# A batched matmul minus a tensor: transfers of two tiles in one fixed order, stores trailing, transposes between the matmuls

## The chip, the cores and the metric

The kernel runs on one core of one Trainium2 chip. The metric is the time on the device in microseconds (us). A kernel's time is the median of its runs. The profile is of one execution.

## The reference

```python
batch, m, k, n = 16, 512, 1024, 768      # x [16,512,1024], weight [1024,768], sub_value [16,512,768], all float32

def reference(x, weight, sub_value):
    return (np.matmul(x, weight) - sub_value).astype(np.float32)
```

The batch and m are flattened: 8192 rows of x, each with 1024 elements, times one weight, less 8192 rows of sub_value. In all 33.55 MB of x, 3.15 MB of weight and 25.17 MB of sub_value are read, and 25.17 MB are written.

## The kernel before

The 8192 rows are cut into 64 tiles of 128 rows. A tile goes through five steps:

- x is loaded as float32 (`load_x_sup`, L76), one DMA for four tiles. Each partition holds four successive rows of x, so a DMA moves 16 KB a partition, 2 MB in all.
- ScalarE casts one tile to float16 (`do_cast`, L104).
- TensorE transposes it in eight blocks of 128 x 128 into a PSUM tile (`do_transpose`, L112), and ScalarE copies that to SBUF as `xt_tile` (L117).
- TensorE multiplies `xt_tile` by the weight (`do_matmul`, L127): first 512 columns of the result, eight matmuls, one for each 128 of k, then the other 256 columns, eight more.
- VectorE subtracts `sub_tile` from the PSUM result into `out_tile` (L136). Once four tiles are done, one DMA stores them (L143). `sub_tile` is loaded by one DMA for four tiles too (L83).

The weight is loaded in eight pieces of 128 rows (L88) through two staging buffers, and VectorE casts each to float16 (L89). All DMAs are issued by SP, and SP takes its instructions in order: where one waits, those behind it wait as well.

The loop runs over the tiles. In it, casts run nine tiles ahead of the matmuls (`C_AHEAD`), transposes six (`T_AHEAD`) and x loads three groups of four (`X_AHEAD`), as far as the buffers allow. The order that the engines get is not quite that of the code: the framework's scheduler places each instruction when it thinks it can run, so weight loads and x loads are mixed on SP, and the transposes of several tiles are put together on TensorE. The framework also gives each DMA one of eight semaphores in turn (`DMAHW0` to `DMAHW7`); a DMA may have to wait for the one that last used the same semaphore, as some rows below show.

Of the kernel before, what the change touches and what calls it, by code (L numbers as in the profile page):

```python
# [1 line left out]

# [5 lines left out]

P = 128
F32 = mybir.dt.float32  # L10
F16 = mybir.dt.float16


@with_exitstack
def kernel(
    ctx: ExitStack,
    tc: tile.TileContext,
    x: bass.AP,
    weight: bass.AP,
    sub_value: bass.AP,  # L20
    out: bass.AP,
):
    nc = tc.nc

    x_flat = x.flatten_outer_dims()
    sub_flat = sub_value.flatten_outer_dims()
    out_flat = out.flatten_outer_dims()

    M_TOT, K = x_flat.shape
    _, N = weight.shape  # L30
    assert M_TOT % P == 0
    assert K % P == 0
    n_mtiles = M_TOT // P
    n_ktiles = K // P

    SUP = 4
    assert n_mtiles % SUP == 0
    n_sup = n_mtiles // SUP

    x_sup_ap = x_flat.rearrange("(s p j) k -> s p j k", p=P, j=SUP)  # L40
    sub_sup_ap = sub_flat.rearrange("(s p j) n -> s p j n", p=P, j=SUP)
    out_sup_ap = out_flat.rearrange("(s p j) n -> s p j n", p=P, j=SUP)

    n_splits = []
    n0 = 0
    while n0 < N:
        w = min(512, N - n0)
        n_splits.append((n0, w))
        n0 += w

    T_AHEAD = 6
    C_AHEAD = 9
    X_AHEAD = 3

    const_pool = ctx.enter_context(tc.tile_pool(name="const", bufs=1))
    w_stage_pool = ctx.enter_context(tc.tile_pool(name="w_stage", bufs=2))
    w_pool = ctx.enter_context(tc.tile_pool(name="w_pool", bufs=1))
    x_pool = ctx.enter_context(tc.tile_pool(name="x_pool", bufs=X_AHEAD + 1))
    x16_pool = ctx.enter_context(tc.tile_pool(name="x16_pool", bufs=6))
    xt_pool = ctx.enter_context(tc.tile_pool(name="xt_pool", bufs=T_AHEAD + 2))  # L60
    sub_pool = ctx.enter_context(tc.tile_pool(name="sub_pool", bufs=3))
    out_pool = ctx.enter_context(tc.tile_pool(name="out_pool", bufs=2))
    psum_t_pool = ctx.enter_context(tc.tile_pool(name="psum_t", bufs=4, space=bass.MemoryType.PSUM))
    psum_o_pool = ctx.enter_context(tc.tile_pool(name="psum_o", bufs=2, space=bass.MemoryType.PSUM))

    identity = const_pool.tile([P, P], F16)
    make_identity(nc, identity)

    w_sb = w_pool.tile([P, n_ktiles, N], F16)

    x_tiles: dict[int, bass.AP] = {}

    def load_x_sup(s):
        t = x_pool.tile([P, SUP, K], F32, tag="x", name="x_tile")
        x_tiles[s] = t
        nc.sync.dma_start(out=t, in_=x_sup_ap[s])  # L76

    sub_tiles: dict[int, bass.AP] = {}

    def load_sub_sup(s):  # L80
        t = sub_pool.tile([P, SUP, N], F32, tag="sub", name="sub_tile")
        sub_tiles[s] = t
        nc.sync.dma_start(out=t, in_=sub_sup_ap[s])  # L83

    load_x_sup(0)
    for kt in range(n_ktiles):
        w_stage = w_stage_pool.tile([P, N], F32, name="w_stage")
        nc.sync.dma_start(out=w_stage, in_=weight[kt * P : (kt + 1) * P, :])  # L88
        nc.vector.tensor_copy(out=w_sb[:, kt], in_=w_stage)  # L89
    for s in range(1, X_AHEAD + 1):  # L90
        if s < n_sup:
            load_x_sup(s)
    load_sub_sup(0)
    if n_sup > 1:
        load_sub_sup(1)

    x16_tiles: dict[int, bass.AP] = {}
    xt_tiles: dict[int, bass.AP] = {}

    def do_cast(mi):  # L100
        s, j = divmod(mi, SUP)
        t = x16_pool.tile([P, K], F16, name="x16_tile")
        x16_tiles[mi] = t
        nc.scalar.copy(out=t, in_=x_tiles[s][:, j])  # L104

    def do_transpose(mi):
        x16_tile = x16_tiles.pop(mi)
        xt_tile = xt_pool.tile([P, n_ktiles, P], F16, name="xt_tile")
        xt_tiles[mi] = xt_tile
        psum_t = psum_t_pool.tile([P, n_ktiles, P], F16, name="psum_t")  # L110
        for kt in range(n_ktiles):
            nc.tensor.transpose(  # L112
                psum_t[:, kt, :],
                x16_tile[:, kt * P : (kt + 1) * P],
                identity,
            )
        nc.scalar.copy(out=xt_tile, in_=psum_t)  # L117

    out_tiles: dict[int, bass.AP] = {}

    def do_matmul(mi):
        s, j = divmod(mi, SUP)
        xt_tile = xt_tiles.pop(mi)
        psum_o = psum_o_pool.tile([P, N], F32, name="psum_o")
        for n0, nw in n_splits:
            for kt in range(n_ktiles):
                nc.tensor.matmul(  # L127
                    psum_o[:, n0 : n0 + nw],
                    xt_tile[:, kt, :],
                    w_sb[:, kt, n0 : n0 + nw],  # L130
                    start=(kt == 0),
                    stop=(kt == n_ktiles - 1),
                )
        if j == 0:
            out_tiles[s] = out_pool.tile([P, SUP, N], F32, name="out_tile")
        nc.vector.tensor_tensor(  # L136
            out=out_tiles[s][:, j],
            in0=psum_o,
            in1=sub_tiles[s][:, j],
            op=mybir.AluOpType.subtract,  # L140
        )
        if j == SUP - 1:
            nc.sync.dma_start(out=out_sup_ap[s], in_=out_tiles.pop(s))  # L143

    for mi in range(min(C_AHEAD, n_mtiles)):
        do_cast(mi)
    for mi in range(min(T_AHEAD, n_mtiles)):
        do_transpose(mi)

    for mi in range(n_mtiles):  # L150
        s, j = divmod(mi, SUP)
        if j == 0:
            if s + X_AHEAD + 1 < n_sup:
                load_x_sup(s + X_AHEAD + 1)
            if s + 2 < n_sup:
                load_sub_sup(s + 2)
        if mi + C_AHEAD < n_mtiles:
            do_cast(mi + C_AHEAD)
        if mi + T_AHEAD < n_mtiles:
            do_transpose(mi + T_AHEAD)  # L160
        do_matmul(mi)


# [1 line left out]
_INS = ['x', 'weight', 'sub_value']  # L165
_OUTS = [((16, 512, 768), 'float32')]


# [23 lines left out]
```

## Time and profile before

| | |
|---|---|
| runs | 228.85, 230.29, 231.27 us; median 230.29 |
| profiled execution: span from first to last instruction | 229.0 us (its own time is not listed beside the three; the median stands 1.3 us above the span) |
| TensorE matmuls | 203.4 us busy, 89% of the span |
| ScalarE / VectorE | 124.0 us (54%) / 65.8 us (29%) |
| DMA | 87.04 MB on SP's queue, its packets 91.1% of 16 engines' span |

Lines of the profile name an engine (PE is TensorE, PEld its weight loads, DVE VectorE, ACT ScalarE, SPq the DMA issues of SP), a line of the kernel and the tiles. A row of the chain of waits has its start in us, its length in us, and what ran; xN says how many instructions are merged. A row of a table of windows has the stretch (from:to and its length), the busy us and instructions of PE, PEld, DVE, ACT and POOL, and at its end the clock that TensorE was granted (1.00 is full), the busy share of the DMA engines and the GB/s that they moved. A row of instructions grouped by line has the busy us, the mean ns of one, the idle us before them and what ended that.

### The profile page before, as it was taken

To read this page: it belongs to the slowest core of one execution; us is meant where nothing else is said; L and a number is where in the kernel's file an instruction comes from. 1 tells how busy PE (TensorE), PEld (TensorE's weight loads), DVE (VectorE), ACT (ScalarE), POOL (GpSimd) and SP (SyncE) were. 2 spreads that over 40 slices of the span, in tenths; PEclk is the share of its full clock that TensorE was granted. 3 is DMA by queue.
4 is the path that set the end of the run, shared out by engine and by line. 5 is a ranking of instruction groups with operands and counts; after the bars stand their busy time and mean duration, and the time that the engine had idled before them with its cause. 6 is when DMAs were issued, how large, how long until landed. Compare 5 with 4: busy or idle time off the path is not lost.

```text
span 229.0 us, 3465 instructions
## 1 busy us (share of the span) xinstructions
PE 203.4 (89%) x1536; PEld 132.6 (58%) x1536; DVE 65.8 (29%) x72; ACT 124.0 (54%) x129; POOL 0.7 (0%) x6
## 2 busy tenths in 40 slices
PE   0259559999999999999999999999999999999970
PEld 0236325666666676666757576667575766666540
DVE  0101113333333331423332413333332413233430
ACT  2499863382583666566583939475656565510000
POOL 1000000000000000000000000000000000000000
PEclk9995967999999999999999999999999999999996
DMA  6999999999999999999999999999999999750606
GB/s 235 421 429 401 427 431 432 419 399 412 352 427 427 439 419 433 425 436 420 430 429 431 423 424 426 431 426 423 429 423 435 424 416 350 305 240 39 271 6 275
DMA packets 8079, 87.26 MB, mean 381 GB/s; under 512 B 896, under 2 KB 896, under 8 KB 1920
## 3 DMA queue, kind: packets, MB, share of 16 engines
q1 hardware_dynamic: 8064, 87.04, 91.1%
q8 instruction: 12, 0.20, 0.3%
q14 instruction: 3, 0.02, 0.0%
HBM read 61.87 MB, written 25.17 MB: 380 GB/s over the span
## 4 chain that ended last, share of the span: by engine, by line
PE 82%; DMA 12%; DVE 1%; ACT 0%; SPq 0%; issue 0%
PE psum_o L127 72%; DMA w_stage<-in_weight_dram 12%; PE psum_t L112 10%; DVE w_sb L89 1%; ACT xt_tile L117 0%; DVE out_tile L136 0%; SPq L88 0%; SPq L76 0%
## 5 line engine op out<-in xcount | busy, mean ns | idle before, releaser
L127 PE MATMUL psum_o<-w_sb,xt_tile 128*128 128x512 f16 (+1 forms) x1024 | 174.7, 330 | 3.6 <-DVE w_sb L89 3.1
L127 PEld LDWEIGHTS <-xt_tile 128*128 128x128 f16 x1024 | 100.1, 99 | 70.3 <-issue 4.6
L117 ACT COPY xt_tile<-psum_t 128x1024 f16<-128x1024 f16 x64 | 63.2, 1016 | 68.9 <-PE psum_t L112 37.6
L136 DVE TENSOR_TENSOR out_tile<-psum_o,sub_tile 128x768 f32<-128x768 f32 x64 | 61.3, 958 | 129.4 <-PE psum_o L127 126.2
L104 ACT CAST x_tile<-x_tile 128x1024 f16<-128x1024 f32 x64 | 63.5, 1053 | 8.8 <-DMA x_tile<-in_x_dram 8.8
L112 PE MATMUL psum_t<-identity,x_tile 128*128 128x128 f16 x512 | 37.4, 230 | 15.1 <-ACT x_tile L104 14.6
L112 PEld LDWEIGHTS <-x_tile 128*128 128x128 f16 x512 | 33.7, 104 | 19.0 <-ACT x_tile L104 16.1
L89 DVE CAST w_sb<-w_stage 128x768 f16<-128x768 f32 x8 | 4.5, 560 | 27.9 <-DMA w_stage<-in_weight_dram 27.9
L104 ACT ACT_TABLE_LOAD x1 | 1.3, 1283 | 0.7 <-PEq L176 0.7
masks.py:199 POOL TENSOR_SCALAR_AFFINE_SELECT identity<-identity 128x128 f16<-128x128 f16 x1 | 0.3, 294 | 0.1
masks.py:197 POOL MEMSET identity<- 128x128 f16 x1 | 0.2, 205 | 0.3 <-POOLq L176 0.3
L176 POOL MEMSET const-bfloat16-1.0<- 128x1 bf16 x1 | 0.1, 102 | 0.0
L176 POOL MEMSET const-uint8-127<- 128x1 uint8 x1 | 0.1, 102 | 0.0
L176 POOL MEMSET const-float32-0.0<- 128x1 f32 x1 | 0.1, 99 | 0.2 <-issue 0.2
L176 POOL MEMSET const-float32-1.0<- 128x1 f32 x1 | 0.1, 99 | 0.0
## 6 DMA issues: line engine op xcount, KB each, us to landing
x_tile<-in_x_dram SPq DMA_DIRECT2D x16, 2048.0 KB, 14.6
sub_tile<-in_sub_value_dram SPq DMA_DIRECT2D x16, 1536.0 KB, 17.8
out_dram<-out_tile SPq DMA_DIRECT2D x16, 1536.0 KB, 10.1
w_stage<-in_weight_dram SPq DMA_DIRECT2D x8, 384.0 KB, 6.3
```

The costliest lines, as they stand in the source:

```text
L89: nc.vector.tensor_copy(out=w_sb[:, kt], in_=w_stage)
L104: nc.scalar.copy(out=t, in_=x_tiles[s][:, j])
L112: nc.tensor.transpose(psum_t[:, kt, :], x16_tile[:, kt * P : (kt + 1) * P], identity,)
L117: nc.scalar.copy(out=xt_tile, in_=psum_t)
L127: nc.tensor.matmul(psum_o[:, n0 : n0 + nw], xt_tile[:, kt, :], w_sb[:, kt, n0 : n0 + nw], start=(kt == 0), stop=(kt == n_ktiles - 1),)
L136: nc.vector.tensor_tensor(out=out_tiles[s][:, j], in0=psum_o, in1=sub_tiles[s][:, j], op=mybir.AluOpType.subtract,)
L176: nc = _bacc.Bacc("TRN2", target_bir_lowering=False, num_devices=1)
```

## The change

A group is now two tiles (`J = 2`), for x, sub and out alike, so a DMA moves 1 MB of x or 0.79 MB of sub or out. The weight is loaded in four pieces of 256 rows (0.79 MB), with as many staging buffers; a partition holds two successive rows of the weight, so block `kt` of k consists of every second row of a piece, and the transposes read every second column of the cast x to match. At the start SP issues x tile 0, weight piece 0, x tile 1 and the other weight pieces, then groups 1 and 2 of x, and so on. For each group g, `transfers(g)` then issues the x load of group g+4, the sub load of g+2 and the store of g-2, in this order. The result is written over `so_tile`, which held sub. The matmuls make 384 + 384 columns in two PSUM banks, both halves for one block of k after each other, and after each such pair one transpose of the tile two ahead follows. Each instruction is wrapped in `keep`, which holds it in the order of the code.

```diff
+J = 2
+D = 6
+TA = 2
+CA = 2
...
-    x_pool = ctx.enter_context(tc.tile_pool(name="x_pool", bufs=X_AHEAD + 1))
-    x16_pool = ctx.enter_context(tc.tile_pool(name="x16_pool", bufs=6))
-    xt_pool = ctx.enter_context(tc.tile_pool(name="xt_pool", bufs=T_AHEAD + 2))
-    sub_pool = ctx.enter_context(tc.tile_pool(name="sub_pool", bufs=3))
-    out_pool = ctx.enter_context(tc.tile_pool(name="out_pool", bufs=2))
-    psum_t_pool = ctx.enter_context(tc.tile_pool(name="psum_t", bufs=4, space=bass.MemoryType.PSUM))
-    psum_o_pool = ctx.enter_context(tc.tile_pool(name="psum_o", bufs=2, space=bass.MemoryType.PSUM))
+    x_pool = ctx.enter_context(tc.tile_pool(name="x_pool", bufs=6))
+    x16_pool = ctx.enter_context(tc.tile_pool(name="x16_pool", bufs=4))
+    xt_pool = ctx.enter_context(tc.tile_pool(name="xt_pool", bufs=4))
+    so_pool = ctx.enter_context(tc.tile_pool(name="so_pool", bufs=11))
+    psum_t_pool = ctx.enter_context(tc.tile_pool(name="psum_t", bufs=2, space=bass.MemoryType.PSUM))
+    psum_o_pool = ctx.enter_context(tc.tile_pool(name="psum_o", bufs=3, space=bass.MemoryType.PSUM))
...
+    def load_w(c):
+        st = w_stage_pool.tile([P, 2, N], F32, name="w_stage")
+        keep(nc.sync.dma_start(out=st, in_=w_c[c]))
+        keep(nc.vector.tensor_copy(out=w_sb[:, c], in_=st))
...
+                c, r = divmod(kt, 2)
+                keep(nc.tensor.transpose(
+                    ps_t[mi][:, kt * P : (kt + 1) * P],
+                    x16_t[mi][:, 2 * P * c + r : 2 * P * (c + 1) : 2],
+                    ident,
+                ))
...
+                for h in range(2):
+                    keep(nc.tensor.matmul(
+                        po_t[mi][:, h, :NS],
+                        lhsT,
+                        w_sb[:, c, r, h * NS : (h + 1) * NS],
+                        start=(kt == 0),
+                        stop=(kt == n_kt - 1),
+                    ))
...
+    def finish(mi):
+        g, j = divmod(mi, J)
+        o = so_t[g][:, j].rearrange("p (h n) -> p h n", h=2)
+        keep(nc.vector.tensor_tensor(
+            out=o, in0=po_t.pop(mi)[:, :, :NS], in1=o, op=mybir.AluOpType.subtract
+        ))
+    load_x(0, 0)
+    load_w(0)
+    load_x(0, 1)
+    for c in range(1, n_c):
+        load_w(c)
+    load_x(1)
+    load_x(2)
+    load_sub(0)
+    load_x(3)
+    load_sub(1)
+    def transfers(g):
+        if g + 4 < n_g:
+            load_x(g + 4)
+        if g + 2 < n_g:
+            load_sub(g + 2)
+        if g - (D - 4) >= 0:
+            store(g - (D - 4))
...
+    for mi in range(n_mt):
+        if mi % J == 0:
+            transfers(mi // J)
+        mm = matmuls(mi)
+        tr = transposes(mi + TA) if mi + TA < n_mt else []
+        per = max(1, n_kt // len(tr)) if tr else 1
+        for kt in range(n_kt):
+            mm[kt]()
+            if tr and kt % per == per - 1:
+                tr.pop(0)()
+        if mi + CA + TA < n_mt:
+            cast(mi + CA + TA)
+        finish(mi)
+    for g in range(n_g - (D - 4), n_g):
+        store(g)
```

SP at the start of the program, before the change. Numbers tell buffers apart; 128x4096 are four tiles of x, 128x768 one of the eight weight pieces, and what a DMA waits for stands in brackets:

```order
L76 DMA x_tile_91<-in_x_dram 128x4096
L88 DMA w_stage_93<-in_weight_dram 128x768
L88 DMA w_stage_96<-in_weight_dram 128x768
L76 DMA x_tile_117<-in_x_dram 128x4096
L88 DMA w_stage_99<-in_weight_dram 128x768 [waits DMAHW1_49,DVE_49]
L88 DMA w_stage_102<-in_weight_dram 128x768 [waits DMAHW2_49,DVE_49]
L76 DMA x_tile_119<-in_x_dram 128x4096
L88 DMA w_stage_105<-in_weight_dram 128x768 [waits DMAHW4_49,DVE_49]
```

The same place after the change; 128x1536 is one of the four weight pieces, or a group of sub:

```order
L82 DMA x_tile_88<-in_x_dram 128x1024
L73 DMA w_stage_90<-in_weight_dram 128x1536
L82 DMA x_tile_88<-in_x_dram 128x1024
L73 DMA w_stage_94<-in_weight_dram 128x1536
L73 DMA w_stage_97<-in_weight_dram 128x1536
L73 DMA w_stage_100<-in_weight_dram 128x1536
L80 DMA x_tile_103<-in_x_dram 128x2048
L80 DMA x_tile_105<-in_x_dram 128x2048
L86 DMA so_tile_107<-in_sub_value_dram 128x1536 [waits DMAHW0_49]
```

The whole weight moved ahead of the second group of x, and no weight load waits any more. From the ninth DMA on, each waits for the one eight before it.

SP further on after the change, where the first stores stand (before the change, the first store stands behind five x loads of four tiles and three sub loads):

```order
L80 DMA x_tile_275<-in_x_dram 128x2048 [waits DMAHW7_49,Activation_49]
L86 DMA so_tile_277<-in_sub_value_dram 128x1536 [waits DMAHW0_49]
L89 DMA out_0_dram<-so_tile_107 128x1536 [waits DMAHW1_49,DVE_49]
L80 DMA x_tile_342<-in_x_dram 128x2048 [waits DMAHW2_49,Activation_49]
L86 DMA so_tile_344<-in_sub_value_dram 128x1536 [waits DMAHW3_49]
L89 DMA out_0_dram<-so_tile_111 128x1536 [waits DMAHW4_49,DVE_49]
```

The x load of group 6 (`x_tile_275`) stands ahead of the store of group 0, and that of group 7 behind it.

TensorE where the first matmuls stand, before the change (`x16_tile` is the cast x, `psum_t` receives transposes, `psum_o` the result; LDWEIGHTS loads the stationary operand):

```order
L112 LDWEIGHTS x16_tile_133
L112 MATMUL psum_t_179<-identity_85,x16_tile_133 128x128
L127 LDWEIGHTS xt_tile_145 [waits Activation_49]
L127 MATMUL psum_o_228<-w_sb_90,xt_tile_145 128x512 [waits DVE_49]
L127 LDWEIGHTS xt_tile_145
L127 MATMUL psum_o_228<-w_sb_90,xt_tile_145 128x512 [waits DVE_49]
L127 LDWEIGHTS xt_tile_156 [waits Activation_49]
L127 MATMUL psum_o_260<-w_sb_90,xt_tile_156 128x512
```

The same place after the change:

```order
L111 LDWEIGHTS x16_tile_126
L111 MATMUL psum_t_128<-ident_82,x16_tile_126 128x128
L130 LDWEIGHTS xt_tile_124
L130 MATMUL psum_o_147<-w_sb_87,xt_tile_124 128x384 [waits DVE_49]
L130 LDWEIGHTS xt_tile_124
L130 MATMUL psum_o_147<-w_sb_87,xt_tile_124 128x384
L111 LDWEIGHTS x16_tile_139 [waits Activation_49]
L111 MATMUL psum_t_150<-ident_82,x16_tile_139 128x128 [waits PE_49]
```

Before, four tiles are transposed ahead and the first two are then multiplied in turn; now two are transposed ahead, and after two matmuls of tile 0 comes a transpose of tile 2 (`x16_tile_139`, cast from `x_tile_103`, which is group 1 of x). This pattern of two matmuls and one transpose goes on to tile 61.

More of the change, by code (lines that the diff above doesn't have):

```diff
@@ L23 @@
     nc = tc.nc
+    keep = tc.keep_in_program_order
     x_flat = x.flatten_outer_dims()
@@ L30 @@
     _, N = weight.shape
[L31 to L49, printed above, removed]
@@ L64 @@
-    psum_o_pool = ctx.enter_context(tc.tile_pool(name="psum_o", bufs=2, space=bass.MemoryType.PSUM))
[L66 to L101, printed above, removed]
-        t = x16_pool.tile([P, K], F16, name="x16_tile")
-        x16_tiles[mi] = t
-        nc.scalar.copy(out=t, in_=x_tiles[s][:, j])
@@ L106, in do_transpose @@
[L106 to L161, printed above, removed]
+    x_pool = ctx.enter_context(tc.tile_pool(name="x_pool", bufs=6))
@@ new lines @@
+    x16_pool = ctx.enter_context(tc.tile_pool(name="x16_pool", bufs=4))
[3 more added lines that the diff above has]
+    psum_o_pool = ctx.enter_context(tc.tile_pool(name="psum_o", bufs=3, space=bass.MemoryType.PSUM))
+    ident = const_pool.tile([P, P], F16)
+    make_identity(nc, ident)
+    w_sb = w_pool.tile([P, n_c, 2, N], F16)
@@ new lines, with load_x @@
+    x_t = {}
+    so_t = {}
+    x16_t = {}
+    xt_t = {}
+    ps_t = {}
+    po_t = {}
+    def load_w(c):
+        st = w_stage_pool.tile([P, 2, N], F32, name="w_stage")
+        keep(nc.sync.dma_start(out=st, in_=w_c[c]))
+        keep(nc.vector.tensor_copy(out=w_sb[:, c], in_=st))
+    def load_x(g, js=None):
+        if g not in x_t:
+            x_t[g] = x_pool.tile([P, J, K], F32, name="x_tile")
+        if js is None:
+            keep(nc.sync.dma_start(out=x_t[g], in_=x_g[g]))
+        else:
+            keep(nc.sync.dma_start(out=x_t[g][:, js], in_=x_g[g][:, js]))
@@ new lines, in load_sub, with store, cast, transposes @@
+    def load_sub(g):
+        so_t[g] = so_pool.tile([P, J, N], F32, name="so_tile")
+        keep(nc.sync.dma_start(out=so_t[g], in_=sub_g[g]))
+    def store(g):
+        keep(nc.sync.dma_start(out=out_g[g], in_=so_t.pop(g)))
+    def cast(mi):
+        g, j = divmod(mi, J)
+        t = x16_pool.tile([P, K], F16, name="x16_tile")
+        x16_t[mi] = t
+        keep(nc.scalar.copy(out=t, in_=x_t[g][:, j]))
+    def transposes(mi):
+        def start():
+            ps_t[mi] = psum_t_pool.tile([P, K], F16, name="psum_t")
+        def fin():
+            xt = xt_pool.tile([P, K], F16, name="xt_tile")
+            xt_t[mi] = xt
+            keep(nc.scalar.copy(out=xt, in_=ps_t.pop(mi)))
+            x16_t.pop(mi)
+        def one(kt):
+            def f():
+                if kt == 0:
+                    start()
+                c, r = divmod(kt, 2)
[4 more added lines that the diff above has]
+                ))
+                if kt == n_kt - 1:
+                    fin()
+            return f
+        return [one(kt) for kt in range(n_kt)]
@@ new lines, in matmuls, with one, f @@
+    def matmuls(mi):
+        def one(kt):
+            def f():
+                if kt == 0:
+                    po_t[mi] = psum_o_pool.tile([P, 2, 512], F32, name="psum_o")
+                c, r = divmod(kt, 2)
+                lhsT = xt_t[mi][:, kt * P : (kt + 1) * P]
+                for h in range(2):
[6 more added lines that the diff above has]
+                    ))
+            return f
+        return [one(kt) for kt in range(n_kt)]
@@ new lines, in finish @@
+    def finish(mi):
+        g, j = divmod(mi, J)
+        o = so_t[g][:, j].rearrange("p (h n) -> p h n", h=2)
[19 more added lines that the diff above has]
+            store(g - (D - 4))
@@ new lines @@
+    for mi in range(TA):
+        cast(mi)
+        for f in transposes(mi):
+            f()
+    for mi in range(TA, CA + TA):
+        cast(mi)
+    for mi in range(n_mt):
[11 more added lines that the diff above has]
+        finish(mi)
```

14 lines of the change are left out of this document (10 added, 4 removed).

## The prediction

> **What bounds the kernel now.** I read the page first, then the chain that ended last in order of time, then the waits and the start of the timeline.
>
> ```profile
> span 229.0 us, 3465 instructions
> PE 203.4 (89%) x1536; PEld 132.6 (58%) x1536; DVE 65.8 (29%) x72; ACT 124.0 (54%) x129; POOL 0.7 (0%) x6
> q1 hardware_dynamic: 8064, 87.04, 91.1%
> PE psum_o L127 72%; DMA w_stage<-in_weight_dram 12%; PE psum_t L112 10%; DVE w_sb L89 1%; ACT xt_tile L117 0%; DVE out_tile L136 0%; SPq L88 0%; SPq L76 0%
> ```
>
> TensorE and the transfers are both near full; the chain lies on TensorE for 82% and on the weight's DMA for 12%. In order of time the chain shows where each is:
>
> ```profile
> 1.64 9.14 DMA w_stage<-in_weight_dram
> ...
> 11.40 6.25 DMA w_stage<-in_weight_dram
> ...
> 18.26 6.26 DMA w_stage<-in_weight_dram
> ...
> 25.13 6.69 DMA w_stage<-in_weight_dram
> 31.85 0.57 DVE w_sb L89
> 32.46 4.44 PE psum_o L127 x18
> ...
> 54.20 0.45 PE psum_t L112 x8
> 54.64 2.60 PE psum_o L127 x16
> ...
> 182.16 1.79 PE psum_t L112 x32
> 183.94 10.40 PE psum_o L127 x64
> ...
> 196.13 26.02 PE psum_o L127 x160
> 222.17 0.96 DVE out_tile L136
> ```
>
> SP's own waits name what holds the weight back:
>
> ```profile
> SPq L88 <- DMA w_stage<-in_weight_dram: 15.9, 3, 7.0
> ```
>
> Until 31.85 us the weight arrives in pairs of 384 KB, each pair waiting on SP for a staging buffer, with a 2 MB x load queued ahead of it. From 32.46 to 222.17 TensorE hardly stops. A tile (128 rows of the result) costs 0.45 + 2.60 = 3.05 us; four at a time cost 1.79 + 10.40 = 12.19, so 3.048 each. All 64 tiles need 195.1 us, and TensorE ends at 222.17: **27.1 us of start-up loss**. The steady part is at the price of its columns (16 matmuls of 384 columns on average, 162.5 ns each; transposes 56 ns each), so the change must win at the start, at the end, or not at all.
>
> **The change, part by part.**
>
> *Start.* What the weight and x cost to arrive is read from the first casts and from the transfer windows:
>
> ```profile
> 8.89 3.88 ACT L104 CAST x_tile<-x_tile 128x1024 f16<-128x1024 f32 x4 [6.87 <-DMA x_tile<-in_x_dram]
> 10.81 0.56 DVE L89 CAST w_sb<-w_stage 128x768 f16<-128x768 f32 x1 [0.40 <-DMA w_stage<-in_weight_dram]
> 16.70 0.56 DVE L89 CAST w_sb<-w_stage 128x768 f16<-128x768 f32 x1 [5.33 <-DMA w_stage<-in_weight_dram]
> 2.00:26.00 24.00, 11.26 (x84) 7.87 (x85) 3.36 (x6) 17.13 (x20) 0.00 (x0) 0.86 0.99 409
> 26.00:46.00 20.00, 16.02 (x108) 9.91 (x107) 4.95 (x6) 9.57 (x10) 0.00 (x0) 0.83 1.00 422
> 46.00:62.00 16.00, 16.00 (x115) 10.04 (x114) 5.75 (x6) 8.90 (x10) 0.00 (x0) 1.00 1.00 384
> 62.00:178.00 116.00, 116.00 (x921) 76.82 (x919) 36.39 (x38) 73.45 (x77) 0.00 (x0) 1.00 1.01 428
> ```
>
> In queue order the second weight piece ends at byte 2.10 + 2 x 0.39 = 2.88 MB and its cast starts at 10.81; the third ends at 2.88 + 2.10 + 0.39 = 5.37 MB and its cast starts at 16.70. That is 423 GB/s. I carry the new order over this line: x tile 0 ends at 0.52 MB (about 5.2 us, by 423 GB/s back from 8.89), the last weight piece at 4.19 MB: 10.81 + 1.31/0.423 = 13.9 us, cast by 15.0 (1536 elements, twice 0.56). Group 1 of x ends at 5.24 MB: 16.70 - 0.13/0.423 = 16.4 us. The new order puts a transpose of tile 2 behind the first two matmuls of tile 0, and TensorE takes its instructions in order, so it stands until group 1 is cast. With these rows,
>
> ```profile
> L104 ACT CAST x_tile<-x_tile 128x1024 f16<-128x1024 f32 x64 | 63.5, 1053 | 8.8 <-DMA x_tile<-in_x_dram 8.8
> L117 ACT COPY xt_tile<-psum_t 128x1024 f16<-128x1024 f16 x64 | 63.2, 1016 | 68.9 <-PE psum_t L112 37.6
> L136 DVE TENSOR_TENSOR out_tile<-psum_o,sub_tile 128x768 f32<-128x768 f32 x64 | 61.3, 958 | 129.4 <-PE psum_o L127 126.2
> L112 PEld LDWEIGHTS <-x_tile 128*128 128x128 f16 x512 | 33.7, 104 | 19.0 <-ACT x_tile L104 16.1
> ```
>
> the steady work starts at 16.4 + 1.05 = **17.45 us**, when the transposes of tiles 0 and 1 and two matmuls are done (0.89 + 0.32 = 1.2 us of the 195.1). The weight's own wait is thereby covered; what is late next is group 1 of x.
>
> Tile 1 of x, ending at 1.84 MB (8.3 us), is cast and transposed by about 10.3; TensorE has then stood for some 7 us. What a restart costs, the clock in the windows shows (the column before the last two):
>
> ```profile
> 30.00:32.00 2.00, 0.95 (x2) 0.25 (x2) 0.71 (x2) 2.00 (x3) 0.00 (x0) 0.56 1.08 445
> 34.00:36.00 2.00, 2.00 (x10) 1.24 (x9) 0.39 (x1) 1.01 (x1) 0.00 (x0) 0.50 1.00 424
> 36.00:38.00 2.00, 1.49 (x14) 1.12 (x12) 1.52 (x2) 1.01 (x1) 0.00 (x0) 0.74 1.03 434
> 38.00:40.00 2.00, 2.00 (x16) 1.18 (x16) 0.00 (x0) 0.00 (x0) 0.00 (x0) 1.00 1.09 465
> ```
>
> The granted clock is 0.50 until about 37 us, 4.5 us after the steady work begins at 32.46 and 6 us after the matmul at 31.05. At half speed that loses 2.3 to 3.0 us; I take 2.6 and keep 0 to 3.0.
>
> TensorE then ends at 17.45 + (195.1 - 1.2) + 2.6 = **213.9 us**, 8.3 earlier.
>
> *The matmuls* (512 + 256 columns become 384 + 384, a transpose after every second). Columns and instruction counts are the same. Each change between transposes and matmuls is unpriced as such, but in the chain one per tile (0.45 + 2.60) and one per four tiles (1.79 + 10.40) both come to 3.05 per tile, so I take nothing for sixteen. One thing has no row: the transposes now load every second column of `x16_tile`, because the weight's rows are paired. A contiguous load shows 104 ns and hides under transposes spaced 56 ns; now it has a 162 ns matmul ahead of it. I take 0, since at the 104 ns of the nearest row it fits; the other end, a load twice as long (208 ns), would leave 46 ns bare. A gain below 0 is excluded, since no gap is left to close.
>
> The Trainium skill, "TensorE: Matmul & The Clock Gate", section "Weight-path perf modes", says that a fast weight load may be packed or strided, with column steps up to 1,024 elements; by it the term is 0, and no run here yet shows a strided load.
>
> *ScalarE, VectorE, PSUM.* ScalarE alternates copy and cast: 1.02 + 1.05 = 2.07 us per 3.05 us tile, and a cast for tile i+4 is due only in tile i+2, so 1 us of slack remains; if that went, TensorE would wait for the rest each tile. Two transpose buffers instead of four are hidden by the same tile of slack. The subtraction in place has as many elements (0.96 us) and hides under TensorE, except the last one. Casting twice as much weight at once costs DVE 1.1 us four times, under the wait for x.
>
> *The transfers.* Same 87.04 MB in 101 pieces of 0.5 to 1 MB, for 56 of up to 2 MB. The page's DMA list has the time to landing:
>
> ```profile
> x_tile<-in_x_dram SPq DMA_DIRECT2D x16, 2048.0 KB, 14.6
> ```
>
> SP now stops at each store for the subtraction of two groups back; behind it stand the x load for four groups ahead and the sub load for two ahead. Each x load is released some five groups (30 us) before its use, against the 14.6 us that a load of twice the size takes to land, so ScalarE does not feel it. Per group of two tiles 2.62 MB move while TensorE needs 6.10 us: 430 GB/s, and the window from 62 us shows 428. So the two keep pace. In queue order x of group 6 ends at 13.6 MB (16.70 + 8.3/0.423 = 36 us) and its transposes are due at about 50; x of group 31 ends at 79.2 MB and is due at about 201.5. To lose that lead takes under 65.6/165 = 397 GB/s. By the end, 87.04 - 9.8 (moved by 26 us) - 0.79 (the last store) = 76.4 MB must pass before 213.9: 407 GB/s. At 428 they are through by 204.6.
>
> What a smaller piece costs is bounded by the windows: 409 GB/s from 2 to 26 us, with eight pieces of 384 KB among the loads, against 428. For 9.8 MB that is 1.1 us, or 0.14 us per small piece as an estimate; 45 more pieces add 6.3 us and end at 211, still before TensorE. The lower end is nothing, and the upper end is the slowest window, 384 GB/s. I take the 0.14.
>
> Against the change speaks the Trainium skill, "DMA: Bandwidth & Descriptors", section "Bandwidth": batch to at least 1 MiB, with 341 GB/s measured there for 1 MB and 425 for 16 MB. At 341 the 87.04 MB alone would take 255 us; the windows with 384 KB pieces at 409 GB/s disagree with that, as queued transfers overlap.
>
> *End.* After the last subtraction:
>
> ```profile
> 223.15 0.33 SPq L143 DMA_DIRECT2D out_dram<-out_tile  x1
> 224.00:225.00 1.00, 0.00 (x0) 0.00 (x0) 0.00 (x0) 0.00 (x0) 0.00 (x0) 0.89 1.16 492
> 227.00:228.00 1.00, 0.00 (x0) 0.00 (x0) 0.00 (x0) 0.00 (x0) 0.00 (x0) 0.50 0.48 197
> ```
>
> From 223.13 to 229.0 there are 5.9 us, most of it the 1.57 MB store. Half of it saves 0.79/0.423 = 1.9; 4.0 remain.
>
> *Sum.* 213.9 + 0.96 + 4.0 = 218.9 us of span, 10.1 under 229.0. The median of the runs, 230.29, stands 1.3 above that span; with it the forecast is **220.2 us**.
>
> **The rivals.**
>
> *The smaller transfers become the bound.* For: the share of the DMA engines is 0.99 or more in the four windows up to 178 us, and one of them shows 384 GB/s. Against: 428 over 116 us, at the demand of TensorE. It decides below 407 GB/s. At 384 all but the last store end at 26 + 76.4/0.384 = 225, and with the tail the run takes 230.3: the gain is eaten whole, and the change would not do what it says. At 400 it is about 222. The batching rule of the Trainium skill ("DMA: Bandwidth & Descriptors", "Bandwidth") is this rival at its worst, and has its chance within it.
>
> *The strided weight load is not hidden (slower).* 62 tiles x 8 = 496 transposes stand between matmuls. The gain of 10.1 us is gone from 20 ns each, that is from a load of 182 ns. At 208 ns it costs 46 x 496 = 22.8 us: 243 us. For it: nothing here shows such a load. Against: it must be 1.75 times the contiguous one.
>
> *The restart is cheap.* If the clock stays at 1.00 over the wait for group 1, 2.6 us fall away: 217.6.
>
> **How the numbers follow.** A measurement of this kernel tells about 1% from no change, 228.0 to 232.6. The forecast with its own spread (216.5 to 223, the cheap restart in it) gets 0.74; the transfer bound 0.14, two thirds of it between 223 and 228; the strided load 0.08; faster than 216.5, by something that I don't see, 0.04. The range 216 to 225 holds the forecast and the milder half of the transfer bound, about 0.8. Faster by over 1%: 0.74 + 0.04 + 0.09 = 0.87; within 1%: 0.05; slower: 0.08.
>
> **What would show it.** Right: the chain leaves the DMA for TensorE at about 17.5 us, TensorE's wait there is on the cast of x and the clock is 0.50 for some 5 us after it; tiles take 3.05 us; transpose plus matmul have no idle time in the middle; TensorE ends near 214 and the last store takes 4 us. Wrong: TensorE waiting for casts whose x lands late (transfers), a tile longer than 3.08 us without waits (weight load), or ScalarE's copy ending waits on TensorE (slack of one tile too thin).

## The result, and the profile after

The changed kernel takes 220.97 us (median of four runs, 220.84 to 221.18), against 230.49 for the kernel before in the runs beside it: 0.959 of the time, 95% interval 0.956 to 0.963. The forecast was 220.2 in a range of 216 to 225. The profiled execution took 220.84 us, its span is 219.1 us; 218.9 was forecast for the span.

The page of the changed kernel, the lines that answer to those shown of before:

```profile
span 219.1 us, 3599 instructions
PE 198.7 (91%) x1536; PEld 130.3 (59%) x1536; DVE 65.1 (30%) x68; ACT 126.9 (58%) x129; POOL 0.7 (0%) x6
q1 hardware_dynamic: 14544, 87.04, 95.7%
PE psum_o L130 77%; PE psum_t L111 13%; DMA x_tile<-in_x_dram 6%; SPq L73 1%; ACT x_tile L95 0%; DVE so_tile L143 0%; SPq L82 0%
```

The weight's DMA is gone from the chain; one x load (6%) stands in its place, and TensorE makes up some 90% (82% before). The same chain in order of time (start, length, what ran):

```profile
4.20 12.44 DMA x_tile<-in_x_dram
16.66 1.05 ACT x_tile L95
18.05 0.64 PE psum_o L130 x2
18.79 0.64 PE psum_o L130 x2
...
24.23 0.33 PE psum_o L130 x2
24.61 0.33 PE psum_o L130 x2
...
208.55 5.21 PE psum_o L130 x32
213.79 0.96 DVE so_tile L143
```

Group 1 of x lands at 16.66 us, its cast ends at 17.7, and from there TensorE runs to 213.79, 8.4 us earlier than the 222.17 of before. The pairs of matmuls first follow each other every 0.74 us and later every 0.38: what was left of the first tile runs at about half speed. From the last subtraction's end at 214.75 to the end are 4.35 us, for 5.87 before.

In the middle one transpose and two matmuls alternate without a gap, eight times a tile:

```profile
61.12 0.06 PE psum_t L111
61.17 0.33 PE psum_o L130 x2
61.50 0.06 PE psum_t L111
61.55 0.33 PE psum_o L130 x2
```

That is 0.381 us a pair and 3.05 us a tile, as before. All that TensorE waits for is casts of x, three times and only up to 17.76 us:

```profile
PE psum_t L111 <- ACT x_tile L95: 15.0, 3, 6.5
```

The transfers in the windows:

```profile
2.00:26.00 24.00, 10.95 (x68) 6.79 (x69) 5.06 (x6) 8.29 (x10) 0.00 (x0) 1.00 1.01 402
62.00:178.00 116.00, 116.00 (x916) 76.63 (x915) 36.39 (x38) 74.41 (x76) 0.00 (x0) 1.00 1.02 423
```

In the long window they move 423 GB/s where it was 428, and TensorE is busy for the whole 116 us.

### The profile page after: what moved, and what is told of

It is laid out like the page before. It is cut to its first block, busy times and chain, and to the rows that moved or that the text cites. A ratio compares the mean times of both kernels' runs of the same rounds, so it can differ in the third digit from the quotient of the medians.

```text
span 219.1 us, 3599 instructions
## 1 busy us (share of the span) xinstructions
PE 198.7 (91%) x1536; PEld 130.3 (59%) x1536; DVE 65.1 (30%) x68; ACT 126.9 (58%) x129; POOL 0.7 (0%) x6
## 3 DMA queue, kind: packets, MB, share of 16 engines
q1 hardware_dynamic: 14544, 87.04, 95.7%
## 4 chain that ended last, share of the span: by engine, by line
PE 89%; DMA 6%; SPq 1%; ACT 0%; DVE 0%; issue 0%
PE psum_o L130 77%; PE psum_t L111 13%; DMA x_tile<-in_x_dram 6%; SPq L73 1%; ACT x_tile L95 0%; DVE so_tile L143 0%; SPq L82 0%
## 5 line engine op out<-in xcount | busy, mean ns | idle before, releaser
L130 PE MATMUL psum_o<-w_sb,xt_tile 128*128 128x384 f16 x1024 | 196.8, 329 | 0.0
L111 PE MATMUL psum_t<-ident,x_tile 128*128 128x128 f16 x512 | 111.2, 223 | 15.0 <-ACT x_tile L95 15.0
L104 ACT COPY xt_tile<-psum_t 128x1024 f16<-128x1024 f16 x64 | 64.8, 1013 | 73.8 <-PE psum_t L111 73.8
L143 DVE TENSOR_TENSOR so_tile<-psum_o,so_tile 128x768 f32<-128x768 f32 x64 | 61.3, 958 | 138.3 <-PE psum_o L130 138.3
L130 PEld LDWEIGHTS <-xt_tile 128*128 128x128 f16 x1024 | 80.0, 99 | 34.5 <-issue 0.8
L111 PEld LDWEIGHTS <-x_tile 128*128 128x128 f16 x512 | 50.4, 100 | 48.6 <-ACT x_tile L95 16.0
L95 ACT CAST x_tile<-x_tile 128x1024 f16<-128x1024 f32 x64 | 67.0, 1049 | 8.3 <-DMA x_tile<-in_x_dram 8.1
L74 DVE CAST w_sb<-w_stage 128x1536 f16<-128x1536 f32 x4 | 3.8, 960 | 11.3 <-DMA w_stage<-in_weight_dram 11.3
```

Source lines behind the costliest of these rows:

```text
L74: keep(nc.vector.tensor_copy(out=w_sb[:, c], in_=st))
L95: keep(nc.scalar.copy(out=t, in_=x_t[g][:, j]))
L104: keep(nc.scalar.copy(out=xt, in_=ps_t.pop(mi)))
L111: keep(nc.tensor.transpose(ps_t[mi][:, kt * P : (kt + 1) * P], x16_t[mi][:, 2 * P * c + r : 2 * P * (c + 1) : 2], ident,))
L130: keep(nc.tensor.matmul(po_t[mi][:, h, :NS], lhsT, w_sb[:, c, r, h * NS : (h + 1) * NS], start=(kt == 0), stop=(kt == n_kt - 1),))
L143: keep(nc.vector.tensor_tensor(out=o, in0=po_t.pop(mi)[:, :, :NS], in1=o, op=mybir.AluOpType.subtract))
```

## The experiments

The ratios are to runs of the kernel before, made beside each group of experiments on the same chip. Their medians lie between 230.34 and 230.61 us, so times are also compared with the changed kernel's 220.97 us directly.

**The weight early, by itself.** In the kernel before:

```diff
-    w_stage_pool = ctx.enter_context(tc.tile_pool(name="w_stage", bufs=2))
+    w_stage_pool = ctx.enter_context(tc.tile_pool(name="w_stage", bufs=8))
```

> The kernel before, with eight staging buffers for the weight instead of two: the weight is then loaded right behind the first x group and is in place at about 17 us (5.24 MB at 423 GB/s). Theory 'the order of the whole start counts': the wait only moves on, since sub of the first group still stands behind three x loads, at 13.1 MB or 35 us, and two result buffers hold two tiles; transposes can be done meanwhile. TensorE goes on at about 36 us, ends near 220 to 222, the run takes 228 to 230. Rival 'the weight alone was the loss': TensorE ends near 214 and the run takes about 222.

Measured: 230.86 us, 1.003 of the kernel before (1.000 to 1.006). A line of its waits, and three of its chain:

```profile
DVE out_tile L136 <- DMA sub_tile<-in_sub_value_dram: 19.1, 1, 19.1
```

```profile
9.59 11.72 DMA x_tile<-in_x_dram
...
35.47 1.98 PE psum_t L112 x16
...
222.13 0.96 DVE out_tile L136
```

With the weight in place at 17 us, VectorE waits 19.1 us for the first sub, and TensorE, whose two result buffers are full, ends at 222.13, as before. Taking away the wait that the chain named gained nothing. The chain of this run does not name sub either: it goes over the second x load (landed at 21.3 us), its casts and copies, and transposes that stand ahead of tile 2's matmuls. Those transposes end at 37.45 us; the first subtraction, which frees a result buffer, ends at 37.08. Two waits end here almost together, and the next run moves one of them.

**The weight and the first sub early.** The same, and sub of the first group ahead of the second x load:

```diff
+    load_sub_sup(0)
     for s in range(1, X_AHEAD + 1):
         if s < n_sup:
             load_x_sup(s)
-    load_sub_sup(0)
```

> As the kernel with eight staging buffers, and the sub load of the first group moved ahead of the second x group. Groups stay at four tiles, the scheduler's order, 512 + 256 columns and the separate result tile stay too. Theory 'the start is the gain, and the rest of the rewrite is worth the smaller last store': TensorE ends at 213 to 216, the last store takes its old 5.9 us, the run 221.5 to 224.5. Rival 'small groups, pinned order or stores that trail carry the gain': it stays above 227.

Measured: 225.25 us, 0.980 (0.974 to 0.986): 5.2 us of the gain, 0.75 us above what I expected and under the rival's 227, so the start is the larger part and something more than the smaller last store is missing. The chain tells where the rest is:

```profile
10.33 14.42 DMA x_tile<-in_x_dram
24.77 3.88 ACT x_tile L104 x4
...
216.51 0.96 DVE out_tile L136
```

Group 1 of x, 2 MB behind 1.6 MB of sub, lands at 24.8 us, and four casts in a row (3.9 us) follow on ScalarE before it turns to the copies. TensorE has tiles 2 and 3 to multiply until 26.2 us; then it waits for such casts and copies in pieces, up to 41.7 us and some 4 us in all. The second sub lands only at 39.3.

**Groups of two as well.** The same kernel with groups of two tiles, buffers for as much sub and result as before (for x 12 tiles instead of 16, as in the changed kernel), and nearly the changed kernel's order of the first loads; the scheduler still places the instructions:

```diff
-    SUP = 4
+    SUP = 2
...
-    load_sub_sup(0)
-    for s in range(1, X_AHEAD + 1):
-        if s < n_sup:
-            load_x_sup(s)
-    if n_sup > 1:
-        load_sub_sup(1)
+    load_x_sup(1)
+    load_x_sup(2)
+    load_sub_sup(0)
+    load_x_sup(3)
+    load_sub_sup(1)
+    load_x_sup(4)
+    load_x_sup(5)
```

> The kernel with the early weight and sub (225.3 us) with groups of two tiles instead of four for x, sub and out, the early loads in the changed kernel's order and buffers for as much as before. The scheduler's order on TensorE, 512 + 256 columns and the separate result tile stay. Theory 'early weight plus groups of two is the whole gain': group 1 of x lands at about 16.5 instead of 24.8 us, the last store halves; TensorE ends at 210 to 213, the run 217 to 221, at or under the changed kernel's 221.0. Rival 'the pinned order or the interleaving carries a part': it stays above 222.5.

Measured: 220.17 us, 0.956 (0.953 to 0.959). Its chain:

```profile
6.67 9.32 DMA x_tile<-in_x_dram
16.02 1.99 ACT x_tile L105 x2
...
213.34 0.96 DVE out_tile L137
```

TensorE ends at 213.34, a little later than the 210 to 213 that I expected, but the time is that of the changed kernel or just under it. Against the run before this one TensorE ends 3.2 us earlier, and from the last subtraction's end to the end of the span are 4.1 us instead of 5.9. So early weight, early sub and groups of two are enough for the whole gain. The pinned order, the transposes between matmuls, 384 + 384 columns and the result over sub add nothing to it in sum. That does not make each of them worth nothing: two experiments further on, the pinned kernel without the mixing takes 216.68 us, 3.5 less than this one, so the mixing costs about what the others bring. Which of the others brings it, no run separated.

**Contiguous weight loads.**

```diff
-    w_c = weight.rearrange("(c p r) n -> c p r n", p=P, r=2)
+    w_c = weight.rearrange("(c r p) n -> c p r n", p=P, r=2)
...
-                    x16_t[mi][:, 2 * P * c + r : 2 * P * (c + 1) : 2],
+                    x16_t[mi][:, kt * P : (kt + 1) * P],
```

> The changed kernel with the weight's rows not paired: its pieces are loaded as two blocks of 128 rows (3 KB runs), and the transposes load 128 contiguous columns of the cast x. Theory 'the strided weight load is hidden': 221.0 within 0.5. Rival 'it costs something': faster, 496 transposes times what each loses (2.5 us at 5 ns).

Measured: 221.58 us, 0.963 (0.958 to 0.969), 0.6 above the changed kernel's median. The weight loads for transposes, in the groups by line, first of the changed kernel, then of this one:

```profile
L111 PEld LDWEIGHTS <-x_tile 128*128 128x128 f16 x512 | 50.4, 100 | 48.6 <-ACT x_tile L95 16.0 <-issue 1.0
```

```profile
L111 PEld LDWEIGHTS <-x_tile 128*128 128x128 f16 x512 | 50.5, 100 | 49.2 <-ACT x_tile L95 16.4 <-issue 1.2
```

Both take 100 ns, and in both a pair of matmuls with its transpose takes 0.38 us, so the step of two elements costs nothing that shows. The 0.6 us, 0.1 outside what I expected, stand at the start: group 1 of x is cast from 17.09 us instead of 16.66, and one pair more runs at half speed after it, which is another 0.37 us. TensorE ends at 214.60 instead of 213.79. That the shorter runs of the weight's loads (3 KB instead of 6) make x later is likely, but no run shows it alone.

**Transposes in a block.**

```diff
         for kt in range(n_kt):
             mm[kt]()
-            if tr and kt % per == per - 1:
-                tr.pop(0)()
+        for f in tr:
+            f()
```

> The changed kernel with the eight transposes of the tile two ahead standing behind the sixteen matmuls of a tile instead of one behind each pair. Theory 'TensorE pays by columns alone': a tile stays at 3.05 us, and at the start tile 0's matmuls no longer stand behind the cast of group 1, but run as the weight's pieces come (last cast ends at 15.1); some 2.3 us of work move ahead of 17.8 us, and the run takes about 218.7. Rival 'mixing transposes and matmuls costs or saves by itself': a tile differs from 3.05 us, by 64 times as much in the run.

Measured: 216.68 us, 0.944 (0.938 to 0.949), 4.3 us under the changed kernel, where I expected 2.3. The timeline of TensorE at the start (start, length, instructions, and in brackets the idle time before):

```profile
10.55 2.36 PE L130 MATMUL psum_o<-w_sb,xt_tile 128*128 128x384 f16 x8
13.39 0.81 PE L130 MATMUL psum_o<-w_sb,xt_tile 128*128 128x384 f16 x4 [0.48 <-DVE w_sb L74]
15.28 0.81 PE L130 MATMUL psum_o<-w_sb,xt_tile 128*128 128x384 f16 x4 [1.08 <-DVE w_sb L74]
17.85 0.62 PE L111 MATMUL psum_t<-ident,x_tile 128*128 128x128 f16 x8 [1.76 <-ACT x_tile L95]
18.30 2.76 PE L130 MATMUL psum_o<-w_sb,xt_tile 128*128 128x384 f16 x16
```

Tile 0's matmuls run as the weight's pieces come, and when group 1 of x is cast TensorE goes on at full speed: 16 matmuls in 2.76 us. TensorE ends at 209.55, 4.24 us earlier. Two things are gained, the 2.3 us of work that moved ahead and some 2 us of half speed. A tile stays at 3.05 us, so mixing or not is neutral by itself; the mixed order cost 4.3 us of the run, all at the start, since the first transpose of tile 2 held up tile 0.

**Work for TensorE while it waits.** The changed kernel with, ahead of its loop:

```diff
+NWARM = 64
...
+    warm = psum_o_pool.tile([P, 2, 512], F32, name="psum_o")
+    for i in range(NWARM):
+        keep(nc.tensor.matmul(warm[:, 0, :P], ident, ident, start=True, stop=True))
```

> The changed kernel with 64 extra matmuls of the identity by itself (128 columns, result not used), placed on TensorE where it stands waiting for group 1 of x, ahead of tile 0's matmuls. They end before that x is cast. Theory 'the first tile after the wait runs at half speed': tile 0 then runs at full speed from the start and TensorE ends some 2.1 us earlier, at about 211.7; the run 218.9. Rival 'the restart is cheap, as the granted clock column (1.00 throughout) says': no change, 221.0, or slower by what the extra work delays.

Measured: 218.79 us, 0.949 (0.946 to 0.951), 2.2 under the changed kernel. The timeline of TensorE:

```profile
10.48 5.68 PE L178 MATMUL psum_o<-ident 128*128 128x128 f16 x64
16.00 0.49 PE L131 MATMUL psum_o<-w_sb,xt_tile 128*128 128x384 f16 x2
17.78 0.23 PE L112 MATMUL psum_t<-ident,x_tile 128*128 128x128 f16 x1 [1.30 <-ACT x_tile L96]
17.85 0.49 PE L131 MATMUL psum_o<-w_sb,xt_tile 128*128 128x384 f16 x2
18.23 0.49 PE L131 MATMUL psum_o<-w_sb,xt_tile 128*128 128x384 f16 x2
```

The work after 17.78 us is the changed kernel's, at the same start, but its pairs follow every 0.38 us from the first on. TensorE's last subtraction starts at 211.76 instead of 213.79. So the half speed is not cheap: its price is 2.0 us of TensorE's time, and the run is 2.2 us shorter.

**Half of the matmuls.** The upper half of k is left out, so the result is not the product:

```diff
+                if kt >= n_kt // 2:
+                    return
                 c, r = divmod(kt, 2)
                 lhsT = xt_t[mi][:, kt * P : (kt + 1) * P]
...
-                        stop=(kt == n_kt - 1),
+                        stop=(kt == n_kt // 2 - 1),
```

> The changed kernel with the matmuls of the upper half of k left out (512 of 1024), all transfers, casts, transposes and subtractions kept. It shows what the transfers alone take. Theory 'TensorE was the bound, the transfers close behind': about 2.4 + 87.04/0.423 = 208 us for the last byte, the run 210 to 212. Rival 'the smaller transfers are the bound': 219 to 221, as before the cut.

Measured: 213.43 us, 0.926 (0.924 to 0.928). Its longest wait and its middle window:

```profile
DVE so_tile L145 <- DMA so_tile<-in_sub_value_dram: 128.4, 32, 6.0
62.00:178.00 116.00, 79.31 (x600) 49.20 (x601) 34.63 (x38) 72.99 (x76) 0.00 (x0) 0.93 1.01 424
```

Here every group waits for its sub, and the transfers still move 424 GB/s. That is what they alone allow: 213.4 us, 1.4 above the 210 to 212 that I expected, and 7.5 under the changed kernel. TensorE was the bound there, with the transfers close behind.

**Stores one group behind.**

```diff
-D = 6
+D = 5
```

> The changed kernel with each store issued one group behind the matmuls instead of two, so x loads run five groups ahead of the stores and not six. Theory 'the distance of the stores is free, since x is some 14 us ahead': 221.0 within 0.5. Rival 'stores that trail by six groups are what keeps loads moving': slower by over 1 us, TensorE waiting for casts.

Measured: 221.12 us, 0.958 (0.955 to 0.961): no difference from the changed kernel. SP's waits for the subtraction grow, from the first line (the changed kernel) to the second (this one):

```profile
SPq L89 <- DVE so_tile L143: 42.2, 18, 5.7
```

```profile
SPq L89 <- DVE so_tile L143: 132.6, 32, 5.7
```

SP waits 90 us longer for subtractions, in part in place of other waits: at the stores it stands 157 us in all instead of 100. No engine feels it. How far the stores trail, a part of the title, is free here between one group and two behind the matmuls; longer and shorter distances were not tried.

**Two tiles first.** The version with the block of transposes, and three edits:

```diff
-    load_x(1)
+    load_x(1, 0)
+    load_x(1, 1)
...
+    transfers(0)
+    mm0, mm1 = matmuls(0), matmuls(1)
+    for kt in range(n_kt):
+        mm0[kt]()
+        mm1[kt]()
+    for mi in range(2):
+        for f in transposes(mi + TA):
+            f()
+        finish(mi)
+        cast(mi + CA + TA)
-    for mi in range(n_mt):
+    for mi in range(2, n_mt):
...
-    for g in range(n_g - (D - 4), n_g):
-        store(g)
+    store(n_g - 2)
+    for j in range(J):
+        keep(nc.sync.dma_start(out=out_g[n_g - 1][:, j], in_=so_t[n_g - 1][:, j]))
```

> The version with transposes in a block (216.7 us), with three edits more: the matmuls of tiles 0 and 1 both stand ahead of the transposes of tile 2, group 1 of x is loaded in two halves, and the last group is stored tile by tile. Theory: 2.6 us more of TensorE's work lie ahead of x's arrival, a wait of 1 us for the copy of tile 2 comes in, the half-sized last store saves 0.9; TensorE ends at 207 to 208, the run takes 213.5 to 215, unless the transfers are the bound by then (they need 422 GB/s and ran at 423). Rival 'the transfers take over': TensorE's result buffers or the last store wait for DMA, the run stays at 215.5 to 217.

Measured: 214.63 us, 0.931 (0.929 to 0.933): the fastest of all, 2.9% under the changed kernel by the medians, and 1.2 us above what the transfers alone took. Its last subtraction, its wait for sub, and a window of its end:

```profile
207.44 0.96 DVE L143 TENSOR_TENSOR so_tile<-psum_o,so_tile 128x768 f32<-128x768 f32 x1 [1.64 <-PE psum_o L130]
DVE so_tile L143 <- DMA so_tile<-in_sub_value_dram: 72.7, 21, 6.0
209.00:211.00 2.00, 0.00 (x0) 0.00 (x0) 0.00 (x0) 0.00 (x0) 0.00 (x0) 1.00 0.63 252
```

TensorE ends at 207.44, inside 207 to 208. The tail is missed: half of the last store was to save 0.9 us, but from 208.40 to the end of the span at 212.9 there are 4.5 us, no less than the changed kernel's 4.35. VectorE already waits 72.7 us for sub, though TensorE does not yet. The last three stores are issued at 202.78, 205.82 and 208.42 us, the last of them while the transfers are still busy; that the earlier ones hold up the last piece is what the window suggests. The halves also go out in runs of 3 KB instead of 6, and no run separated the two.

## Why the prediction was right

**What bounds the kernel.** Right. The half-matmul run puts the transfers' own time at 213.4 us and the changed kernel at 221.0, so TensorE and its start decided, as read from the 27.1 us of start-up loss.

**The start.** Group 1 of x was put at 16.4 us and came at 16.66; TensorE's work was to go on at 17.45 and did at 17.76. That the next thing late would be this load and not the weight is what the chain of the changed kernel shows. The first experiment shows more: the weight's wait, 12% of the chain before, was worth nothing alone, since the second x load and the first sub stood behind it. My sum took x and the weight in their new order, but it has no term for the first sub. The changed kernel's first subtraction, and that of the block version below it, whose first loads are the same:

```profile
22.69 0.96 DVE L143 TENSOR_TENSOR so_tile<-psum_o,so_tile 128x768 f32<-128x768 f32 x1 [7.56 <-PE psum_o L130]
21.18 1.82 DVE L143 TENSOR_TENSOR so_tile<-psum_o,so_tile 128x768 f32<-128x768 f32 x2 [5.96 <-DMA so_tile<-in_sub_value_dram]
```

In the second row sub is what came last, at some 21.1 us; in the changed kernel it came 1.6 us before it was needed. That it would not be the next wait was right without being worked out, which is luck.

**The restart.** 2.6 us were taken from bounds of 0 and 3.0; the experiment with extra work gives 2.0 for TensorE and 2.2 for the run. Half speed came as forecast, but that it is the price of having stood for 7 us is not shown here. The pairs of matmuls before and after the wait:

```profile
10.44 0.85 PE L130 MATMUL psum_o<-w_sb,xt_tile 128*128 128x384 f16 x2
17.84 0.85 PE L130 MATMUL psum_o<-w_sb,xt_tile 128*128 128x384 f16 x2
```

They are equally slow, so TensorE, with 2.7 us of work behind it, had not come to full speed before the wait either. In the kernel before it had (eight transposes in 0.62 us at 27.69), and there a shorter wait was enough:

```profile
31.05 1.01 PE L127 MATMUL psum_o<-w_sb,xt_tile 128*128 128x512 f16 x2 [2.74 <-DVE w_sb L89]
```

The sign that I named, a clock of 0.50 in the windows, did not come in the changed kernel. The windows of the changed kernel say

```profile
18.00:20.00 2.00, 2.00 (x10) 1.00 (x8) 0.00 (x0) 0.65 (x1) 0.00 (x0) 1.00 1.02 420
22.00:24.00 2.00, 2.00 (x17) 1.30 (x16) 0.96 (x1) 1.25 (x2) 0.00 (x0) 1.00 1.03 423
```

with 1.00 in both, and ten instructions in the one against seventeen in the other. The spacing of the matmuls showed the half speed, and the clock column did not. By that column the rival of the cheap restart (217.6 us) would have been right.

**The matmuls.** Nothing was taken for mixing, and a tile costs 3.05 us mixed and in a block. The strided weight load was to cost 0, with a rival at 243 us; it measures 100 ns, as does the contiguous one. The rule of the Trainium skill, "TensorE: Matmul & The Clock Gate", "Weight-path perf modes", that a fast weight load may be strided, agrees with this row. Where the prediction stopped short is the place of the mixing: it saw that the transpose of tile 2 would hold TensorE until 17.45 us, but counted that as given. The block version shows that it was a choice, worth 4.3 us.

**The transfers.** Extra pieces were priced at 0.14 us each, 6.3 us in all. From 428 to 423 GB/s is 2.4 us over 87.04 MB, or 0.05 us for each of 45 pieces as an estimate: nearer the lower bound. It may be more, since before the change TensorE set the pace (430 GB/s by the prediction's count), and no run shows what the larger pieces do alone. Nothing of it reached TensorE. The slowest window of before, 384 GB/s from 46 to 62 us, has 421 now. The Trainium skill, "DMA: Bandwidth & Descriptors", "Bandwidth", has 341 GB/s for 1 MB and the rule to batch to at least 1 MiB; these queued transfers, most of them of 0.75 and 1 MB, moved 423 GB/s, so its figure is not a bound here.

**The end.** 4.0 us were forecast and 4.35 came, 1.5 saved instead of 1.9. In sum TensorE's end was forecast at 213.9 and came at 213.79, but that closeness is luck, since two errors offset each other there: the start 0.3 late, the restart 0.6 cheaper. The run stands 1.7 us above its span where 1.3 was taken. The 1.3 set a median beside the span of another execution; in every run on record, those of the kernel before too, the time is 1.7 to 1.9 us above that run's own span. That and the tail are the 0.8 us between 220.2 and 220.97.

## What to carry to other kernels

When the chain of waits names one late load, put all first uses in queue order with their bytes and read off when each lands: the wait moves to the next load in the queue, and taking away only the named one may give nothing. In an order written by hand, no instruction that needs a late load should stand ahead of one that could run; here one transpose placed too early cost 4.3 us of the 7.5 between the changed kernel and what the transfers allow. And measure what the second bound allows by leaving out work of the first, since it tells when to stop: 213.4 us here, with 214.6 reached.

## What the runs showed of the hardware

- After 2.7 us of work at half speed and a wait of 6.5 us, TensorE ran at half speed for another 4 us (pairs every 0.74 us, then 0.38), while the granted clock in the windows read 1.00.
- In the kernel before, a wait of 2.74 us, up to 31.05 us, took TensorE from full speed (eight transposes in 0.62 us) to half, with a granted clock of 0.56 and then 0.50. After a wait of 1.76 us, in the block version, it went on at full speed.
- Matmuls whose result nobody uses are enough to bring TensorE to full speed: 64 of 128 columns, run in the wait, brought the 2.2 us back.
- Transfers of mostly 0.75 and 1 MB, eight in flight, moved 423 GB/s, against 428 for twice the size where TensorE set the pace.
